# Down projection of the SwiGLU block: residual loads of a closing task ordered behind the first square sum of their tile group

## The chip, the cores and the metric

The kernel runs on one core of one Trainium2 chip. Five engines take part: TensorE (PE, with its weight loads as PEld), VectorE (DVE), ScalarE (ACT), GpSimd (POOL) and SyncE (SP), which issues nearly all of the DMAs here. The metric is the device time of one execution in microseconds. The kernel before took 3222.1 us (median of three runs, 3218.2 to 3226.84). The execution that was profiled took 3209.03 us.

## The reference

Two decoder layers run over 1024 positions of width 1024: a token mixer (gated spatial mixing in layer 0, an RWKV-7 recurrence in layer 1), a cross attention into 256 memory rows, and a SwiGLU block. Each is wrapped as `x + rms_norm(f(rms_norm(x)))`. The change lies in the SwiGLU block's second product and in the sum that follows it:

```python
def swiglu_ffn(x, w_in, w_out):
    gate, up = jnp.split(x @ w_in, 2, axis=-1)
    return (jax.nn.silu(gate) * up) @ w_out        # 2816 -> 1024

h = swiglu_ffn(rms_norm(x, g[4]), ffn_w_in[i], ffn_w_out[i])
x = x + rms_norm(h, g[5])                          # the "residual" is this x
```

## The kernel before

Products run in a split form: an operand is cut into a high and a low part (ACT casts, DVE subtracts: `split`, lines 118 and 119), and three matmuls of the parts replace one. In the SwiGLU block each product is further arranged as seven block products (a Strassen-like scheme). `ffn` (line 440) computes the hidden activations with the matmuls of L438, and `out(m)` inside it writes them to DRAM by SP in pieces `hd[1]` to `hd[7]` (L485 to L501; L490 and L491 store two of them for the last block before anything of the next part can be computed from it).

`ffn_out` (line 556 on) is the down projection. It goes through the products in the order 1, 2, 5, 6, 3, 7, 4, each in six steps (`steps`), with the matmuls of L639. For each step `load` fetches a piece of the hidden activations into a `wr` buffer (L596; there are three, and a buffer comes free when the low part of its split is done) and, in the first four products, a piece of `w_out` into an `a` buffer (L600). `evac` and `finish` take a product's result out of PSUM (L662 to L674), square and sum it on ACT (L651) and multiply it by the gain (L652). The output has eight row tiles of 128 rows. They close in groups: two tiles in layer 0 (`nn` is 2), one tile in layer 1. Even tiles get their first square sum at the end of product 2 and their last at the end of product 3. Odd tiles get them at the end of 7 and of 4. In layer 1 the last product runs tile by tile (`by_tile`).

When a group has all its square sums, `finish` puts a closing task in a queue: `close` (line 363). It loads the old rows of x, the residual, into `t` buffers (L369; there are four), forms the norm factor (L228 on DVE, L208 on POOL), adds the normed result to the residual (L378, DVE), stores the new rows (L379), and in layer 0 squares, scales and transposes them for the next block (L220, L389, L391, L262).

The order on each engine isn't the order of this code. A scheduler simulates the program and moves an instruction ahead when what it depends on is there. A residual load depends on nothing but a free `t` buffer and the rows of x in DRAM, so it may stand far ahead of the task that asks for it. SP issues in its order: where an issue waits, those behind it wait too.

After layer 0's down projection come the key and value product of the memory (L148 to L150, 256 columns wide) and then the recurrence of layer 1: `rwkv_prep` (L1318 to L1354), `rwkv_merge` (L1416, L1425) and `rwkv_chunks` (L1439, L1452), in four batches.

Of the kernel before, what the change touches and what calls it, by code (L numbers as in the profile page):

```python
# [21 lines left out]
class Trunk:  # L22
# [332 lines left out]
    def closer(self, gpost_row, xin, xout, gpre):  # L355

        nc = self.nc
        gpost = self.gain_bc(gpost_row)
        ready = [{}, {}]
        self.xT, self.hF = ({}, [])  # L360
        fp32_in, s7_in = (self.fp32_in, self.s7_in)

        def close(tiles, hs, s):

            n = len(tiles)
            xr = []
            for t in tiles:
                xr.append(self.tmp())
                nc.sync.dma_start(xr[-1], xin[t * P:(t + 1) * P, :])  # L369
            yield  # L370
            r = self.rms(s, n)
            yield
            s, s3 = self.sums(n)
            for i, t in enumerate(tiles):
                m = 2 if gpre is None and t == NT - 1 else 1
                for j in range(m):
                    js = slice(j * D // m, (j + 1) * D // m)
                    nc.vector.scalar_tensor_tensor(out=xr[i][:, js], in0=hs[i][:, js], scalar=r[:, i:i + 1], in1=xr[i][:, js], op0=ALU.mult, op1=ALU.add)  # L378
                    nc.sync.dma_start(xout[t * P:(t + 1) * P, js], xr[i][:, js])  # L379
                if gpre is not None:  # L380
                    self.sumsq(s3[:, :, i], xr[i])
                yield
            if gpre is None:
                return
            r = self.rms(s, n)
            yield
            for i in range(n):
                if 'avav'[i % 4] == 'a':
                    nc.scalar.activation(hs[i], xr[i], AF.Copy, scale=r[:, i:i + 1])  # L389
                else:  # L390
                    (nc.vector if 'avav'[i % 4] == 'v' else nc.gpsimd).tensor_scalar_mul(hs[i], xr[i], r[:, i:i + 1])  # L391
            yield
            half = tiles[0] // 4
            ready[half].update(zip(tiles, hs))
            if len(ready[half]) < 4:
                return
            self.fp32_in = fp32_in
            yield from (self.turn7 if s7_in else self.turn)(half, [ready[half][t] for t in sorted(ready[half])], gpre)
            ready[half] = None
        close.gpost, close.follow = (gpost, gpre is not None)  # L400
        return close
# [177 lines left out]
    def ffn_out(self, hd, w_out, mk_close, late):  # L579

        nc = self.nc
# [6 lines left out]
        y = {}  # L588
        close = mk_close()
# [43 lines left out]
        def mm(ps, q, j):  # L633
# [3 lines left out]
            for k in range(steps[n][1]):  # L637
                for z, (a, b) in enumerate(((hh[:, k, js], wh[:, k]), (hh[:, k, js], wl[:, k]), (hl[:, k, js], wh[:, k]))):
                    nc.tensor.matmul(ps, lhsT=a, rhs=b, start=i in (1, 2, 5) and n == 0 and k == 0 and z == 0, stop=n == NS - 1 and k == steps[n][1] - 1 and z == 2, skip_group_check=True)  # L639
        sums, done = ({}, {})  # L640

        def finish(t, c, src):

            group = (t % 2, t // 2 // nn)
            tiles = [2 * (group[1] * nn + g) + group[0] for g in range(nn)]
            if group not in sums:
                sums[group] = self.sums(nn)
                done[group] = 0
            s, s3 = sums[group]
            o = y[t][:, c * 512:c * 512 + 512]  # L650
            nc.scalar.activation(self.junk, src, AF.Square, scale=1.0 / 32, accum_out=s3[:, c:c + 1, tiles.index(t)])  # L651
            (nc.gpsimd if src is o else nc.vector).tensor_mul(o, src, close.gpost[:, c * 512:c * 512 + 512])  # L652
            done[group] += 1
            if done[group] == 2 * nn:
                self.later(close(tiles, [y[x] for x in tiles], s))

        def evac(i, j, A, B):
            o = lambda r, c: y[2 * j + r][:, c * 512:c * 512 + 512]
            if i in (1, 5):
                y[2 * j + i // 5] = self.a32()  # L660
            if i == 1:
                nc.scalar.copy(o(0, 0), A)  # L662
            elif i == 2:
                nc.vector.tensor_add(o(0, 0), B, o(0, 0))
                finish(2 * j, 0, o(0, 0))
            elif i == 5:
                nc.scalar.copy(o(1, 1), B)
            elif i == 6:
                nc.scalar.copy(o(0, 1), A)
            elif i == 3:  # L670
                nc.vector.tensor_add(o(0, 1), B, o(0, 1))
                finish(2 * j, 1, o(0, 1))
            elif i == 7:
                nc.vector.tensor_add(o(1, 1), A, o(1, 1))  # L674
                finish(2 * j + 1, 1, o(1, 1))
            else:
                finish(2 * j + 1, 0, A)
# [1055 lines left out]
```

## Time and profile before

| | |
|---|---|
| median of three runs | 3222.1 us (3218.2 to 3226.84) |
| profiled execution: time, span | 3209.03 us, 3207.3 us |
| mean granted TensorE clock | 0.972 |
| PE busy, share of the span | 3071.3 us, 96% |
| DVE, ACT, POOL busy | 57%, 46%, 28% |
| down projection, layer 0 | about 1082 to 1304 us of the span |
| recurrence batches, layer 1 | about 1800 to 2200 us |
| down projection, layer 1 | about 2979 us to the end |

PE is busy in nearly the whole span, so time is lost or won where PE waits, or where its granted clock is at the lower of its two levels. Other engines' idle time costs nothing in itself.

### The profile page before, as it was taken

To read this page: it belongs to the slowest core of one execution; us is meant where nothing else is said; L and a number is where in the kernel's file an instruction comes from. 1 tells how busy PE (TensorE), PEld (TensorE's weight loads), DVE (VectorE), ACT (ScalarE), POOL (GpSimd) and SP (SyncE) were. 2 spreads that over 40 slices of the span, in tenths; PEclk is the share of its full clock that TensorE was granted. 3 is DMA by queue.
4 is the path that set the end of the run, shared out by engine and by line. 5 is a ranking of instruction groups with operands and counts; after the bars stand their busy time and mean duration, and the time that the engine had idled before them with its cause. 6 is when DMAs were issued, how large, how long until landed. Compare 5 with 4: busy or idle time off the path is not lost. (4 is left out here: it accounts for less than half of the span.)

```text
span 3207.3 us, 44170 instructions
## 1 busy us (share of the span) xinstructions
PE 3071.3 (96%) x16570; PEld 2511.4 (78%) x16570; DVE 1829.9 (57%) x2674; ACT 1484.9 (46%) x2751; POOL 893.0 (28%) x762
## 2 busy tenths in 40 slices
PE   8999999999999999999989999999999899999998
PEld 6888888778888777878767788887788678888776
DVE  5553544574555476654775677654545755554566
ACT  5433544543333345666763355455545533333443
POOL 0100011365555200111331443333011555554001
PEclk9999999999999999999999889989999999999999
DMA  5622545413333643644867643535544233333634
GB/s 189 207 79 66 190 123 167 151 59 100 104 99 102 226 165 132 204 141 136 255 216 186 188 110 104 146 96 178 181 158 142 94 102 99 99 99 115 236 109 141
DMA packets 432502, 456.56 MB, mean 142 GB/s; under 512 B 77664, under 2 KB 307200, under 8 KB 432288
## 3 DMA queue, kind: packets, MB, share of 16 engines
q1 hardware_dynamic: 425376, 428.57, 42.1%
q0 software_dynamic: 6912, 25.17, 2.5%
q8 instruction: 131, 2.15, 0.3%
q14 instruction: 83, 0.68, 0.1%
HBM read 331.43 MB, written 122.22 MB: 141 GB/s over the span
## 5 line engine op out<-in xcount | busy, mean ns | idle before, releaser
L438 PE MATMUL ps<-a,wh 128*128 128x512 f32 x2464 | 772.0, 398 | 7.0 <-DVE a L119 4.8
L119 DVE TENSOR_TENSOR wl<-wr,wh 128x1024 fp32r<-128x1024 f32 (+1 forms) x417 | 477.6, 1155 | 480.1 <-ACT wh L118 477.3
L118 ACT CAST wh<-wr 128x1024 fp32r<-128x1024 f32 (+1 forms) x417 | 371.1, 901 | 621.3 <-PE ps L639 172.3
L438 PEld LDWEIGHTS ps<-a,wh 128*128 128x128 f32 x2464 | 465.3, 189 | 125.0 <-DVE a L119 7.1
L438 PE MATMUL ps<-a,wl 128*128 128x512 f32 x1232 | 480.2, 398 | 0.0
L148 PE MATMUL ps<-a,wh 128*128 128x512 f32 (+1 forms) x848 | 328.3, 392 | 11.2 <-ACT a L118 7.9
L149 PE MATMUL ps<-a,wh 128*128 128x512 f32 (+1 forms) x848 | 324.7, 384 | 2.4 <-DVE a L119 2.4
L208 POOL TENSOR_TENSOR sm<-sm,mhalf 128x4 f32<-128x4 f32 (+3 forms) x60 | 71.2, 1189 | 914.7 <-DVE sm L228 841.8
L148 PE MATMUL ps<-wh,a 128*128 128x512 f32 x800 | 314.5, 401 | 11.7 <-ACT t L1168 3.0
L150 PE MATMUL ps<-a,wl 128*128 128x512 f32 (+1 forms) x848 | 323.7, 383 | 1.5 <-DVE wl L119 1.5
L149 PE MATMUL ps<-wl,a 128*128 128x512 f32 x800 | 318.1, 398 | 0.8 <-DVE wl L119 0.8
L150 PE MATMUL ps<-wh,a 128*128 128x512 f32 x800 | 316.6, 399 | 0.0
L438 PEld LDWEIGHTS ps<-a,wl 128*128 128x128 f32 x1232 | 233.0, 189 | 57.2 <-DVE wl L119 0.9
L639 PE MATMUL ps<-wl,wh 128*128 128x512 f32 x588 | 231.9, 394 | 11.9 <-DVE wl L119 11.9
L119 DVE TENSOR_TENSOR wl<-s,wh 128x512 fp32r<-128x512 f32 x176 | 199.8, 1149 | 67.5 <-ACT wh L118 64.2
L639 PE MATMUL ps<-wh,wl 128*128 128x512 f32 x588 | 229.9, 391 | 0.0
L639 PE MATMUL ps<-wh 128*128 128x512 f32 x588 | 194.8, 394 | 13.2 <-ACT wh L118 13.2
L118 ACT CAST wh<-s 128x512 fp32r<-128x512 f32 x176 | 106.4, 620 | 199.7 <-PE ps L438 66.7
L148 PEld LDWEIGHTS ps<-a,wh 128*128 128x128 f32 x848 | 162.1, 192 | 44.3 <-ACT a L118 8.8
L150 PEld LDWEIGHTS ps<-a,wl 128*128 128x128 f32 x848 | 162.1, 191 | 35.7 <-DVE wl L119 2.8
L148 PEld LDWEIGHTS ps<-wh,a 128*128 128x128 f32 x800 | 151.3, 189 | 48.5 <-ACT t L1168 3.5
L149 PEld LDWEIGHTS ps<-a,wh 128*128 128x128 f32 x848 | 162.7, 192 | 32.6 <-DVE a L119 2.7
(281 smaller groups left out, 5426.2 us busy)
## 6 DMA issues: line engine op xcount, KB each, us to landing
scr<-a SPq DMA_DIRECT2D x218, 256.0 KB
wr<-in_ffn_w_in SPq DMA_DIRECT2D x90, 512.0 KB
wr<-scr SPq DMA_DIRECT2D x70, 512.0 KB
scr<-t SPq DMA_DIRECT2D x60, 512.0 KB
wr<-in_rw_w_rkv SPq DMA_DIRECT2D x48, 512.0 KB
a<-in_ffn_w_out SPq DMA_DIRECT2D x40, 512.0 KB
t<-scr SPq DMA_DIRECT2D x36, 512.0 KB
ld<-scr SPq DMA_DIRECT2D x72, 256.0 KB
```

The lines of the kernel that those rows point to most:

```text
L118: self.nc.scalar.copy(hi, src)
L119: (engine or self.nc.vector).tensor_sub(lo, src, hi)
L148: nc.tensor.matmul(out, lhsT=ah, rhs=bh, start=start, stop=False)
L149: nc.tensor.matmul(out, lhsT=ah, rhs=bl, start=False, stop=False)
L150: nc.tensor.matmul(out, lhsT=al, rhs=bh, start=False, stop=stop)
L208: self.nc.gpsimd.tensor_tensor(out=r, in0=v, in1=self.mhalf[:, 0:n], op=ALU.pow)
L438: self.nc.tensor.matmul(out, lhsT=a, rhs=b, start=start and k == 0 and (i == 0), stop=k == 3 and i == 2, skip_group_check=True)
L639: nc.tensor.matmul(ps, lhsT=a, rhs=b, start=i in (1, 2, 5) and n == 0 and k == 0 and z == 0, stop=n == NS - 1 and k == steps[n][1] - 1 and ...
```

## The change

`finish` remembers the column of the small tile into which the first square sum of a group goes, and hands it to `close`. There VectorE copies that column (128 x 1) into the first column of each `t` buffer, ahead of the load that overwrites the whole buffer. The load therefore comes after the copy, and the copy after the square sum of L651. Closing tasks of the other blocks pass no column and are as they were. There are 8 such copies in each layer's down projection, 16 in all. In the changed kernel all lines behind `close`'s loop have numbers that are two higher, and those behind `finish` three higher: L369, L485, L596 and L600 are there L371, L487, L598 and L602; L1318 to L1452 are L1321 to L1455.

```diff
-        def close(tiles, hs, s):
+        def close(tiles, hs, s, begun=None):
...
                 xr.append(self.tmp())
+                if begun is not None:
+                    nc.vector.tensor_copy(xr[-1][:, 0:1], begun)
                 nc.sync.dma_start(xr[-1], xin[t * P:(t + 1) * P, :])
...
-        sums, done = ({}, {})
+        sums, done, begun = ({}, {}, {})
...
                 done[group] = 0
+                begun[group] = sums[group][1][:, c:c + 1, tiles.index(t)]
...
-                self.later(close(tiles, [y[x] for x in tiles], s))
+                self.later(close(tiles, [y[x] for x in tiles], s, begun[group]))
```

What the scheduler makes of it is seen in three places. The first is SP's queue at the passage from the hidden activations to the down projection of layer 0 (`scr_93` is x, `scr_4980` to `scr_4986` are `hd`). Before:

```order
L596 DMA wr<-scr_4980 128x2x512 x2
L369 DMA t_9240<-scr_93 128x1024
L485 DMA scr_4980<-a 128x512
L596 DMA wr<-scr_4980 128x2x512
L369 DMA t_9242<-scr_93 128x1024
L369 DMA t_9332<-scr_93 128x1024
L490 DMA scr_4981<-a 128x512
L491 DMA scr_4983<-a 128x512
L600 DMA a<-in_ffn_w_out 128x512
```

Changed:

```order
L598 DMA wr<-scr_4980 128x2x512 x2
L487 DMA scr_4980<-a 128x512
L598 DMA wr<-scr_4980 128x2x512
L492 DMA scr_4981<-a 128x512
L493 DMA scr_4983<-a 128x512
L602 DMA a<-in_ffn_w_out 128x512
L497 DMA scr_4984<-a 128x512
```

The three residual loads are gone from here, and a fourth one, 14 rows further on, is gone too; the four stand some 30 rows later, between the hidden pieces of product 5. The rest keeps its order: the two stores still stand ahead of the first piece of `w_out`. Layer 1 has the same rows and the same move.

The second place is SP's queue near the end of layer 1's down projection (`scr_21280` and `scr_21277` are `hd[7]` and `hd[4]` before, `scr_21288` and `scr_21285` in the changed kernel; the stores are to the output). Before:

```order
L369 DMA t_25889<-scr_96 128x1024
L379 DMA out<-t_25577 128x1024
L596 DMA wr<-scr_21280 128x2x512
L369 DMA t_25933<-scr_96 128x1024
L379 DMA out<-t_25612 128x1024
L379 DMA out<-t_25656 128x1024
L596 DMA wr<-scr_21277 128x512
L369 DMA t_25977<-scr_96 128x1024
L369 DMA t_26021<-scr_96 128x1024
L596 DMA wr<-scr_21277 128x2x512 x5
```

Changed:

```order
L381 DMA out<-t_25586 128x1024
L598 DMA wr<-scr_21288 128x2x512
L381 DMA out<-t_25622 128x1024
L381 DMA out<-t_25667 128x1024
L598 DMA wr<-scr_21285 128x512
L598 DMA wr<-scr_21285 128x2x512 x5
L371 DMA t_25901<-scr_96 128x1024
L371 DMA t_25946<-scr_96 128x1024
L371 DMA t_25991<-scr_96 128x1024
L371 DMA t_26036<-scr_96 128x1024
```

The four last residual loads move from among the hidden pieces of products 7 and 4 to behind all of them.

The third place is on PE, in the third of the four recurrence batches, about where its chunk recurrence begins (L1452, changed L1455: state products; L1330, L1337 and L1354, changed L1333, L1340 and L1357: preparation of the next batch). Before:

```order
L1354 MATMUL ps<-uv,bk 64x64 x16
L1318 MATMUL ps<-sel,ld 128x2 x4
L1330 MATMUL ps<-ar,bk 128x128 x4
L1425 MATMUL ck<-z_14126,x1t 32x32
L1452 MATMUL ck<-s,ar 128x128 x3
L1330 MATMUL ps<-ar,bk 128x128 x4
```

Changed:

```order
L1357 MATMUL ps<-uv,bk 64x64 x8
L1428 MATMUL ck<-z_14134,x1t 32x32
L1357 MATMUL ps<-uv,bk 64x64
L1321 MATMUL ps<-sel,ld 128x2 x4
L1357 MATMUL ps<-uv,bk 64x64 x7
L1333 MATMUL ps<-ar,bk 128x128 x4
L1455 MATMUL ck<-s,ar 128x128 x3
L1333 MATMUL ps<-ar,bk 128x128 x4
```

The recurrence of this batch begins behind another 32 preparing matmuls of 64x64. The code of the recurrence is the same in both kernels: the scheduler's choices there shift with what came before. Of the 48 preparing matmuls of 64x64 that stood behind the start of this batch's recurrence 16 are left; in the first batch it is 16 instead of 32, in the second 48 instead of 32. PE has 14,412 matmul rows of order in both kernels.

## Rows read from the trace of the kernel before

**Rows 1.** The page: span, PE, and the chain that ended last.
```profile
span 3207.3 us, 44170 instructions
PE 3071.3 (96%) x16570; PEld 2511.4 (78%) x16570; DVE 1829.9 (57%) x2674; ACT 1484.9 (46%) x2751; POOL 893.0 (28%) x762
```
**Rows 2.** Timeline of SP, layer 0 passage: start us, us, engine line op.
```profile
1055.95 0.42 SPq L369 DMA_DIRECT2D t<-scr  x1
...
1062.19 12.23 SPq L369 DMA_DIRECT2D t<-scr  x2
1076.60 0.32 SPq L490 DMA_DIRECT2D scr<-a  x1
1076.97 0.42 SPq L491 DMA_DIRECT2D scr<-a  x1
1077.49 0.41 SPq L600 DMA_DIRECT2D a<-in_ffn_w_out  x1
```
**Rows 3.** Waits of SP, 1060 to 1080 us: total, times, longest.
```profile
SPq L369 <- POOL a L549: 11.3, 1, 11.3
...
SPq L490 <- DVE a L558: 2.1, 1, 2.1
```
**Rows 4.** Timelines of DVE, ACT and PE, the same passage; idle and releaser in brackets.
```profile
1075.88 0.69 DVE L558 TENSOR_TENSOR a<-t,ps 128x512 f32<-128x512 f32 x1 [2.73 <-issue]
...
1081.45 0.62 ACT L118 CAST wh<-a 128x512 fp32r<-128x512 f32 x1 [7.63 <-DMA a<-in_ffn_w_out]
...
1082.12 2.07 PE L639 MATMUL ps<-wh 128*128 128x512 f32 x4 [6.43 <-ACT wh L118]
...
1086.42 1.07 PE L639 MATMUL ps<-wh 128*128 128x512 f32 x4
```
**Rows 5.** Timeline of PE, the same passage in layer 1.
```profile
2979.06 2.07 PE L639 MATMUL ps<-wh 128*128 128x512 f32 x4 [6.42 <-ACT wh L118]
```
**Rows 6.** Timeline of SP, last products of layer 1.
```profile
3145.10 0.32 SPq L369 DMA_DIRECT2D t<-scr  x1
3145.59 1.53 SPq L379 DMA_DIRECT2D out<-t  x2
3148.00 0.33 SPq L596 DMA_DIRECT2D wr<-scr  x1
3150.66 1.56 SPq L369 DMA_DIRECT2D t<-scr  x2
3153.92 11.88 SPq L596 DMA_DIRECT2D wr<-scr  x5
```
**Rows 7.** The chain that ended last, in order of time, two stretches.
```profile
1998.85 2.37 DMA a<-scr
...
3148.00 4.47 DMA wr<-scr
...
3153.92 4.62 DMA wr<-scr
...
3162.03 4.64 DMA wr<-scr
...
3169.73 30.57 PE ps L639 x132
```
**Rows 8.** Timeline of PE, 3128 to 3170 us: rows with idle time before them.
```profile
3162.51 1.20 PE L639 MATMUL ps<-wh 128*128 128x512 f32 x4 [0.34 <-ACT wh L118]
3164.33 0.50 PE L639 MATMUL ps<-wl,wh 128*128 128x512 f32 x1 [0.62 <-DVE wl L119]
3169.73 0.50 PE L639 MATMUL ps<-a 128*128 128x512 f32 x1 [0.53 <-DVE a L674]
```
**Rows 9.** Timeline of DVE, the end of layer 1.
```profile
3173.66 0.68 DVE L652 TENSOR_TENSOR a<-a,gb 128x512 f32<-128x512 f32 x1
...
3184.62 1.29 DVE L378 SCALAR_TENSOR_TENSOR t<-a,sm,t 128x1024 f32<-128x1024 f32 x1 [0.66 <-POOL sm L208]
```
**Rows 10.** L228, 3130 to 3208 us: duration in ns, min/median/max, first and last start.
```profile
L228 DVE SCALAR_TENSOR_TENSOR sm<-sm x8: 150/152/156, 3133.6 to 3201.7; 128x1 f32<-128x1 f32 x8
```
**Rows 11.** Chain, recurrence of the last batch: a group of 42 at either clock level.
```profile
2154.80 6.00 PE ck L1439 x42
...
2164.73 3.51 PE ck L1439 x42
...
2170.81 3.51 PE ck L1439 x42
```
**Rows 12.** Windows: us, busy us of PE, PEld, DVE, ACT, POOL, PEclk, DMA share, GB/s.
```profile
1680.00:1840.00 160.00, 145.95 (x1107) 120.69 (x1106) 96.56 (x227) 60.16 (x104) 39.99 (x66) 0.91 0.69 192
1840.00:2000.00 160.00, 155.01 (x1692) 131.62 (x1691) 111.53 (x355) 84.83 (x249) 64.39 (x83) 0.89 0.38 102
2000.00:2200.00 200.00, 194.26 (x2044) 162.33 (x2044) 110.00 (x290) 101.66 (x286) 67.52 (x70) 0.90 0.43 118
```

## The prediction, made before the changed kernel ran

> **What bounds the kernel now.** I read the page first. PE is busy for 3071.3 of 3207.3 us [rows 1], so only what lengthens or shortens PE's own stretch can move the time. Then I looked at the two places in which the moved loads stand, with the timelines of SP, DVE, ACT and PE side by side, and last at the stretch of the recurrence, whose order moves though its code doesn't.
>
> At the passage into the down projection SP looks badly blocked. A pair of residual loads holds its queue for 12.23 us [rows 2], and 11.3 us of that is a wait for POOL's L549, the last reader of the `t` buffer [rows 3]. Behind that pair stand two stores of hidden activations and the first piece of `w_out`. PE waits 6.43 us in layer 0 and 6.42 us in layer 1 for the cast of just that piece [rows 4, 5]. So it is tempting to book the block as the cause of the wait. The reader is to look one row further: the store L490 starts at 1076.60, not at 1074.4 when the pair is through, and it waits for DVE's L558 [rows 3], which runs from 1075.88 for 0.69 us, to 1076.57 [rows 4]. L490 needs the last block of hidden activations, which PE and DVE finish no sooner. The residual pair is waited out inside a wait that stands anyway.
>
> At the end of layer 1 the chain that ended last runs through three loads of hidden pieces, of 4.47, 4.62 and 4.64 us, and then through 30.57 us of unbroken PE work [rows 7]. Two residual issues stand right among them in SP's queue [rows 6]. There DMA does reach PE.
>
> **The passages: what goes and what is late next.** Four residual loads leave each passage. SP's queue then goes from the hidden piece straight to L490, which still waits until 1076.57, and L491 and the `w_out` piece follow as before, at 1076.97 and 1077.49 [rows 2]. The load that was issued last, near 1074.4, has some 2 us before L490 starts and 3 us before the `w_out` piece, so little of it is still on the DMA engines; its share in the 3.96 us between the issue at 1077.49 and the cast at 1081.45 [rows 2, 4] is between 0 and, if it were all still in the way, half of that, 2 us. I take 0, since the two stores of 256 KB ahead of that piece and the loads behind it remain. For both layers that is 0, with 0 to -4 us for the range.
>
> **The end of layer 1.** Four residual loads move behind all hidden pieces. Without them the loads of 4.47 and 4.62 us have two stores beside them, and not these and two residual loads. The nearest short row of a load in the chain is 2.37 us [rows 7], for a smaller piece, so each may shrink by up to 2.2 us, and by nothing at worst. PE can take back only what it waits there: 0.34, 0.62 and 0.53 us [rows 8], 1.49 us in all. Even half of the 4.3 us on the loads covers that, so I take -1.5 us, with 0 as the other end. What is late next is PE itself: it has its 132 matmuls of the last product whatever the loads do.
>
> The moved loads have to be there for L378. In the tail the copies can run when VectorE has done the first gain product of each odd tile, at 3173.66 plus 0.68 for the first [rows 9]. With 0.4 us of issue [rows 2] and the longest load of the chain, 4.64 us [rows 7], the first residual is there at 3179.4; its L378 starts at 3184.62 [rows 9]. That is 5.2 us of cover, and the later tiles have more. In the even tiles the load goes out in product 5 and is used after product 3, three products later. If the cover were gone, each us of lateness in the last tile would be a us of the time; in the others PE would not notice.
>
> **The copies.** Sixteen copies of 128 x 1 are added on VectorE. Its nearest row is L228, also 128 x 1, at 0.152 us [rows 10]; 16 of them are 2.4 us. Most lie in VectorE's idle time. Some stand between the gain products and the splits that PE waits for next (six such places: the ends of products 2 and 7 in both layers, two of them twice). With two copies of 0.15 us on half of these I take +0.6 us. The ends are 0 and +2.4. Queued behind a copy that waits for ACT's square sum are VectorE's next evacuations and splits; but in the order each copy stands behind the gain product of the same or a later tile, when ACT's sum is already there, so I add no wait.
>
> **The recurrence.** Nothing is added or removed there, but PE's order changes in three of the four batches: the recurrence starts behind 32 more preparing matmuls in the third batch, 16 more in the first and 16 fewer in the second. The number of matmuls is the same. A price can't be read directly; I bound it by the clock. A group of 42 matmuls takes 3.51 us at the full level and 6.00 us at the lower one, and the period from one group to the next goes with it from 6.08 us (2164.73 to 2170.81) to 9.93 us (2154.80 to 2164.73) [rows 11]. One group per reordered batch that falls to the lower level, or rises from it, is 3 x 3.85 = 11.6 us, to either side. There is room for both: over 1840 to 2200 us the granted clock is about 0.9 and PE is busy in 349 of 360 us [rows 12], so it is at the lower level for about a fifth of the time. I take 0: two batches begin later, one earlier, and the work is the same.
>
> Here the Trainium skill has a rule that speaks against a reordering that opens gaps: TensorE: Matmul & The Clock Gate, section HAM oscillation, says that waits between bursts of matmuls make the engine slow down again, so that a gap costs more than its own length. The 2.07 us for four matmuls right after the 6.43 us wait, against 1.07 us for the same four later [rows 4], agree with it. By that rule the sum would lean to the slow side if the later starts open gaps, and would stay where it is if they only change places.
>
> **The sum.** On the profiled execution's own time: 3209.0 + 0 (passages) - 1.5 (tail) + 0.6 (copies) + 0 (recurrence) = 3208.1 us, a change of -0.9. That execution ran 13 us below the median of the runs, so I put the change on the median: 3222.1 - 0.9 = 3221 us.
>
> **Rivals.** *The block was the cause after all.* If the freed SP queue did let the first pieces of `w_out` go early, both waits of 6.4 us would go, and with them the slow restart, about 2 us each (1 us on the four matmuls just named, and as much on the next ones): 17 us, 3205 us. For it speaks the 12.23 us; against it that L490 stands ahead of the `w_out` piece in both orders and waits for L558.
>
> *The recurrence gets worse.* A later start leaves more of the recurrence without preparing matmuls to fill its pauses, and the clock falls: 11.6 us, 3233 us. It decides the result from about 10 us on, that is from two or three groups of 42 at the lower level. For it speaks that the two batches with later starts outnumber the one with an earlier start, and that the last batch, which has no filling, is where the slow groups stand now [rows 11]; against it that PE is busy throughout.
>
> *The recurrence gets better.* The same price with the other sign: 3209 us. For it: the lower level takes a fifth of that stretch, and less interleaving could also mean fewer breaks.
>
> *The moved loads come late.* If the copies waited long in VectorE's queue, the last residual would hold the last L378; with 5 us of cover at the first tile and more than 20 at the last this needs a delay that no row shows. The time would still be within a few us of 3222.
>
> **Chances.** My forecast, no change that can be seen, 0.62 (own range 3215 to 3228, the spread of single runs and the small terms); the block was the cause 0.07; recurrence worse 0.17; better 0.12; late loads 0.02, which I count as no change. A measurement here can tell about 0.3%, 9.7 us, from no change. With that, faster by more is 0.19, within 0.64, slower by more 0.17. The range that should hold the time 8 times in 10 reaches into both recurrence cases: 3210 to 3233 us.
>
> **What would show it.** In the changed profile: SP's long issue of residual loads gone at both passages, yet L490 (there L492) still starting right behind L558 and PE still waiting about 6.4 us; at the end of layer 1 the first two loads of the last product under 4 us and PE's three small waits gone; the last residuals landing before 3184. Wrong would be a wait at the passages of 4 us or less (then the block was the cause), or a recurrence stretch whose length moves by more than 5 us, which would set the result alone.

## The result and the profile after

The changed kernel is slower: 3241.42 us (median of 20 executions, 3223.34 to 3259.34) against 3223.6 us for the kernel before in the same sessions (3212.82 to 3249.73, 20 executions). The ratio is 1.0052, with a 95% interval of 1.0034 to 1.0070. The prediction was 3221 us and no change; the time lies above its range.

Where the change was made, the profile after looks as predicted. First the sixteen copies, as the page of line L370 gives them (duration in ns, min/median/max, first and last start):

```profile
L370 DVE COPY t<-sm x16: 143/150/160, 1144.3 to 3211.8; 128x1 f32<-128x1 f32 x16
```

SP's queue at layer 0's passage, then what the store waits for (total, times, longest), then PE's waits for the first `w_out` piece in layer 0 and in layer 1:

```profile
1062.49 0.36 SPq L598 DMA_DIRECT2D wr<-scr  x1
1077.35 0.33 SPq L492 DMA_DIRECT2D scr<-a  x1
1077.74 0.43 SPq L493 DMA_DIRECT2D scr<-a  x1
1078.27 0.38 SPq L602 DMA_DIRECT2D a<-in_ffn_w_out  x1
```
```profile
SPq L492 <- DVE a L560: 14.4, 1, 14.4
```
```profile
1082.81 2.08 PE L641 MATMUL ps<-wh 128*128 128x512 f32 x4 [6.40 <-ACT wh L118]
3013.93 2.07 PE L641 MATMUL ps<-wh 128*128 128x512 f32 x4 [5.87 <-ACT wh L118]
```

The residual block of 12.23 us is gone [rows 2], and nothing came of it. The wait that was booked on the residual loads, 11.3 us, and the 2.1 us of the store behind them [rows 3] stand now as one wait of 14.4 us in the store's name. PE's waits are 6.40 and 5.87 us, against 6.43 and 6.42 [rows 4, 5].

At the end of layer 1 the four last residual loads stand behind all hidden pieces (SP), behind the copy, and are there before the first L380 asks for them (DVE, which waits only for POOL's factor):

```profile
3184.07 15.30 SPq L598 DMA_DIRECT2D wr<-scr  x6
3207.14 5.18 SPq L371 DMA_DIRECT2D t<-scr  x4
```
```profile
3206.96 0.15 DVE L370 COPY t<-sm 128x1 f32<-128x1 f32 x1
3217.42 1.29 DVE L380 SCALAR_TENSOR_TENSOR t<-a,sm,t 128x1024 f32<-128x1024 f32 x1 [0.66 <-POOL sm L208]
```

PE waits there once, for 2.72 us at 3177.06, which the kernel before also does (2.71 us at 3141.01); the three small waits of [rows 8] are gone. The first load of the last product is cast 2.8 us after its issue (3184.07 to 3186.90), where it was 4.55 (3148.00 to 3152.55). From the matmul behind the wait of 2.7 us to the end it is 66.3 us before and 64.0 after. That gain of 2.3 us doesn't show in the larger stretch, from the first matmul of layer 1's hidden product to the end (689.7 us before, 2517.62 to 3207.3, and 689.8 after, 2551.26 to 3241.1), since this execution had lost about as much before that matmul.

Up to 1580 us, behind all that layer 0's half of the change moves, PE's records in the two profiles stay within 2 us of each other.

The time went in the recurrence, which no line of the change touches. The four batches, each from the start of its merge to the next (us, PE busy and records, granted clock, DMA share, GB/s), before and after:

```profile
1821.60:1900.90 79.30, 74.12 (x964) 0.91 0.45 123
1900.90:2009.20 108.30, 104.48 (x1137) 0.85 0.44 118
2009.20:2131.50 122.30, 118.77 (x1232) 0.97 0.50 135
2131.50:2197.30 65.80, 65.79 (x733) 0.77 0.23 68
```
```profile
1827.00:1914.00 87.00, 76.13 (x964) 0.88 0.43 116
1914.00:2026.00 112.00, 108.53 (x1136) 0.83 0.43 114
2026.00:2159.90 133.90, 130.53 (x1233) 0.86 0.45 123
2159.90:2226.00 66.10, 66.10 (x733) 0.77 0.23 68
```

375.7 us became 399.0. In the first batch PE is idle for 5.7 us more (10.9 against 5.2); in the second and third it is busy all the same, with as many records, at a lower granted clock. These 23.3 us are the larger part of the 33.8 us between the two spans; 5.4 us more lie ahead of the first merge, which starts anywhere from 1821.6 to 1830.3 us in executions of the order of before. One execution of each can't say which of these differences is the order's and which is chance. That took the experiments.

### The profile page after: what moved, and what is told of

The parts are those of the page before. It is cut to its first block, busy times and chain, and to the rows that moved or that the text cites. A ratio compares the mean times of both kernels' runs of the same rounds, so it can differ in the third digit from the quotient of the medians.

```text
span 3241.1 us, 44205 instructions
## 1 busy us (share of the span) xinstructions
PE 3095.0 (95%) x16570; PEld 2530.7 (78%) x16570; DVE 1835.8 (57%) x2690; ACT 1484.3 (46%) x2751; POOL 889.7 (27%) x762
## 5 line engine op out<-in xcount | busy, mean ns | idle before, releaser
L641 PE MATMUL ps<-wl,wh 128*128 128x512 f32 x588 | 232.2, 395 | 11.5 <-DVE wl L119 11.3
```

## The experiments

All ratios are to the kernel before on the same chip, with 95% intervals; 12 executions of each kernel, 35 of the kernel before per session.

**One layer at a time.** Layer 1 alone:

```diff
-                self.later(close(tiles, [y[x] for x in tiles], s, begun[group]))
+                self.later(close(tiles, [y[x] for x in tiles], s, None if close.follow else begun[group]))
```

> Only layer 1's closing tasks get the column; layer 0 and the recurrence stand in the order of before on every engine, and layer 1's last product in that of the changed kernel. Theory A (the loss comes from the recurrence, whose order follows from layer 0's half of the change): ratio to before 1.000, at most 0.0005 lower (the 1.5 us of the three waits in the tail), and recurrence batches as in before, the first with about 2.5 us of idle PE. Theory B (the later loads and the copies cost where they stand): half of the loss, 1.0026.

Measured: 0.9985 (0.9959 to 1.0012). In its profile PE is idle in the first batch for 4.8 us, near the 5.2 us of the kernel before, and not about 2.5.

Layer 0 alone:

```diff
-                self.later(close(tiles, [y[x] for x in tiles], s, begun[group]))
+                self.later(close(tiles, [y[x] for x in tiles], s, begun[group] if close.follow else None))
```

> Only layer 0's closing tasks get the column; everything up to layer 1's last product stands in the changed kernel's order on every engine. Theory A: the whole loss, ratio 1.005 (3240 us), with the first recurrence batch some 7 us longer by a PE wait of about 6 us for VectorE's mask product, and the third longer at a lower clock. Theory B: half of it, 1.0026.

Measured: 1.0058 (1.0028 to 1.0087). The whole loss comes with layer 0's half, and theory B, which shares it between the layers, falls. Of the two details expected, the third batch came (148.7 us, clock 0.77), the first did not: 82.2 us.

**The order alone, with the loads left as they are.** Eight small copies on ScalarE at the start of layer 1's mixer shift the scheduler's choices. In the changed kernel:

```diff
         nc = self.nc
+        nc.scalar.copy(self.junk[:, 0:128], self.ident)
...
         B = [self.rwkv_batch() for _ in range(4)]
```

> The changed kernel with 8 small ScalarE copies (128x128, into the unused square tile) ahead of layer 1's mixer. They cost nothing that PE waits for (8 x 0.2 us on ScalarE), but the order of the second half of the recurrence comes out another way: the third batch begins behind 24 preparing matmuls of 64x64 instead of 48; the first batch keeps the changed order. If the first batch's start costs by its order and the third by its own: the first batch keeps its 7 us, the third loses its 11.5 us, ratio 1.0015 to 1.003. If the third batch's length is chance of the clock or follows from the first: 1.005. If the copies' nudge does nothing and layer 0's loads cost: 1.005 with the first batch at 79 us.

Measured: 1.0002 (0.9974 to 1.0029). The same eight lines in the kernel before:

> The kernel before with the same 8 small ScalarE copies. Residual loads as before. The first batch keeps the order of before (16 preparing matmuls of 64x64 ahead), the second and third begin behind 25 each instead of 32 and 16. If the recurrence's order sets the time whatever the loads do: the first batch 79 us with 2.5 us idle, and a time that moves by the length of the second and third, anywhere from 0.998 to 1.005; if only the loads matter: 1.000 and batches as in before.

Measured: 1.0048 (1.0022 to 1.0073). This pair decides against the loads: with the whole change in place the loss can vanish, and without any of it, it can come. In detail the expectation of the nudged changed kernel was only half met: the ratio lies below each of the three that were named, the third batch stayed at 131.7 us, and the second was shorter (105.4 us). In the nudged kernel before the first batch came as expected (79.5 us), and the second and third took 114.8 and 134.0 us.

**The third batch alone.** One 64x1 copy in the changed kernel that depends on a late step of the second batch:

```diff
             nc.scalar.copy(uvc, u)
+            if (b, c4, p) == (1, 3, 0):
+                for _ in range(1):
+                    nc.vector.tensor_copy(self.small(1)[0:64], uvc[:, 0:1])
```

> The changed kernel with one VectorE copy of a 64x1 column more, which waits for a late step of the second batch's recurrence. Every engine keeps the changed order up to there (the first batch and nearly all of the second); the third batch then begins behind 16 preparing matmuls of 64x64, as in the kernel before, instead of 48. Theory A (the order of the third batch sets most of the loss, by the granted clock): the third batch falls from 134 to 149 us to about 122, and the ratio to before from 1.005 to 1.000 to 1.002. Theory B (the loss comes from layer 0's loads, or the first two batches): 1.004 to 1.006, with a third batch of 130 us or more.

Measured: 0.9994 (0.9973 to 1.0014). The loss is gone, with the loads, the copies, and the order of every engine up to late in the second batch as in the changed kernel. The third batch did not come down to 122 us but to 130.2: the ratio is that of theory A, the length that of theory B, and the table below shows how far the third batch accounts for it.

**Is it the count of preparing matmuls ahead?** In the kernel before:

```diff
             nc.scalar.copy(uvc, u)
+            if (b, c4, p) == (0, 3, 0):
+                for _ in range(1):
+                    nc.scalar.copy(self.junk[0:64, 0:128], uvc)
```

> The kernel before with one small ScalarE copy (64x128) more, late in the first batch's recurrence. The loads stand as before; the third batch begins behind 32 preparing matmuls of 64x64 instead of 16, and the end of the first batch is a little otherwise. If the number of preparing matmuls ahead of the third batch sets its length: 130 us or more for it and a ratio of 1.002 to 1.004. If not: 122 us and 1.000.

Measured: 0.9987 (0.9964 to 1.0010). The premise did not come true: PE's 16,570 records in the profile of this kernel stand in the order of the kernel before, one for one by name and shape, with the same 369 from the third merge to the first state product (L1452), in 21.1 us. So the run says nothing on the count of preparing matmuls, which stays untested. It is a repeat of the order of before, with the same time. Its one profile was a long execution (3236.54 us, against a median of 3217.68), with 133.4 us for the third batch: that order, too, can have a long third batch. What I counted from here on is the time and PE's records from the third merge to its first state product.

**Does denser work hold the clock?** Ahead of each merge, here in the changed kernel, then in the kernel before:

```diff
+        for i in range(8):
+            nc.tensor.matmul(pb[i % 4], lhsT=self.chunk_on[:, 0:128], rhs=self.chunk_on, start=True, stop=True)
         for h in range(2):
             for c in range(8):
```

> The changed kernel with 8 bf16 matmuls (128x512, of a constant by itself, overwritten at once) ahead of each merge of the recurrence, 32 in all, of about 0.22 us each: 7 us of added work, part of it in pauses ahead of the merges. The order moves too: 32, 16 and 16 preparing matmuls ahead of the batches. If the lower clock after the merges comes from thin PE work around them and denser work holds the clock: the low stretches that start at the merges (73 to 82 us of lost time in the two profiles with the changed order) shrink by 20 us or more, ratio 0.998 to 1.000. If the fill does nothing for the clock: as the third-batch kernel plus up to 7 us, 1.002 to 1.005.

Measured: 1.0016 (0.9999 to 1.0034). That lies between the two ranges. It can't be set against the changed kernel, because its third batch was put in another order as well. Against the third-batch kernel, which has as many records (401) from the third merge to its first state product, its median is 8.0 us longer, about the added work.

> The kernel before with the same 32 filling matmuls; the batches begin behind 16, 32 and 16 preparing matmuls as before. If denser work around the merges holds the clock: 0.994 to 0.998, with less than 40 us lost to the lower level between the mixer and the end of the recurrence (51 and 53 us in the two profiles with this order). If it does nothing: up to 7 us of added work, 1.000 to 1.002.

Measured: 1.0008 (0.9988 to 1.0028), with 54.5 us lost to the lower level in its profile, not under 40. Its mean clock over the executions is 0.9683 against 0.9669, and its added work takes back as much. But the order moved here too: 401 records and 35.6 us stand from the third merge to its first state product, not 369 and 21.0. So neither filled kernel tests the filling by itself; in neither does it show a gain.

**More executions of the same orders.** To tell order from chance, the changed kernel twice more and the kernel before twice more:

> The changed kernel, profiled once more, for where in the recurrence the lower clock lies. If the third batch's order sets the loss: the third batch again 130 us or more, with 30 us or more at the lower level in it. If the place is chance: its loss lies in another batch.

> As the run before it: third batch 130 us or more if its order sets the loss; another place if the place is chance.

> The kernel before, profiled once more. If the third batch's order sets the loss: its third batch again about 122 us, with some 10 us at the lower level behind its merge. If the place is chance: 130 us or more in one of the two repeats.

> As the run before it: 122 us if the order sets it; the other batches may move by 10 us to either side, as they did between the two profiles of this order so far (the fourth 65.8 and 57.2 us).

and the third-batch kernel twice more:

> The third-batch kernel, profiled once more. Its one profile had a third batch of 130.2 us, between the means of the order of before (122.9 us of four profiles) and of the changed one (140.2 us of four). If the third batch's order takes the loss away by its own length: 122 to 131 us again, and never near 148.7. If its time was even for another reason: 134 us or more here and other batches shorter.

> As the run before it: a third batch of 122 to 131 us if its own order takes the loss away.

With the layer-1 kernel and the kernel with one more ScalarE copy (the recurrence's order is that of before in both) and the layer-0 kernel (the changed order) there are five profiles of the order of before, four of the changed one, and three of the third-batch kernel. Length of each batch, us (the fifth value of the order of before is the long execution just named):

| batch | order of before | changed order | third-batch kernel |
|---|---|---|---|
| first | 79.3, 84.8, 87.8, 88.2, 90.4 | 87.0, 82.2, 83.9, 82.8 | 79.1, 83.6, 82.1 |
| second | 108.3, 106.1, 106.6, 104.6, 106.6 | 112.0, 114.9, 105.7, 107.3 | 107.2, 107.4, 101.4 |
| third | 122.3, 122.1, 121.6, 125.4, 133.4 | 133.9, 148.7, 129.4, 148.7 | 130.2, 129.5, 129.7 |
| fourth | 65.8, 57.2, 67.2, 61.6, 70.1 | 66.1, 57.6, 66.2, 57.5 | 63.8, 62.2, 55.1 |
| mean of the sum | 381.9 | 396.0 | 377.1 |

The third batch is the one that differs most: means of 125.0 and 140.2 us, 15.2 us apart, where the medians of the executions are 17.8 us apart. Its values overlap in one profile, the 133.4 us. The first batch's longer idle time in the changed kernel's profile is no part of it. The second batch's mean is 3.5 us longer in the changed order, on values that overlap. The third-batch kernel's sum is 18.9 us below the changed one's; 10.4 us of that lie in the third batch, the rest in batches whose values overlap.

Two expectations of the repeats fell short: the first repeat of the changed kernel had 129.4 us, not 130, with 23.6 us at the lower level, not 30, and the second of the kernel before had 125.4 us, not 122, with a second stretch of 10 us at the lower level.

The third batch, cut at its first state product, in the kernel before, the changed one and the layer-0 kernel (columns as above):

```profile
2009.20:2030.20 21.00, 21.00 (x369) 0.81 0.63 162
2030.20:2131.50 101.30, 97.77 (x866) 1.00 0.47 129
```
```profile
2026.00:2072.00 46.00, 45.62 (x529) 0.75 0.65 182
2072.00:2159.90 87.90, 84.92 (x706) 0.92 0.35 92
```
```profile
2020.10:2080.60 60.50, 60.21 (x529) 0.53 0.51 146
2080.60:2168.80 88.20, 85.12 (x705) 0.93 0.32 84
```

In the changed order 160 more records stand ahead of the state products, and 160 fewer behind. Work only changed places, and the part behind is 13 us shorter. But the part ahead is 25.0 and 39.5 us longer, since it runs at a low granted clock. Length times granted clock, an estimate of the same work at the full level, is 17.0 + 101.3 = 118.3 us before, 34.5 + 80.9 = 115.4 us in the changed kernel, 32.1 + 82.0 = 114.1 us in the layer-0 kernel. By that estimate the changed order would be no longer at one clock. The repeats fall on the same two lengths, 46.4 and 60.5 us; the order of before gives 20.9 to 21.5 us every time.

In the layer-0 kernel, around the second fall (columns as above, then PE's rows there):

```profile
2020.10:2045.00 24.90, 24.61 (x276) 0.50 0.60 170
2045.00:2049.00 4.00, 4.00 (x30) 0.93 0.35 108
2049.00:2093.00 44.00, 44.00 (x282) 0.50 0.35 99
2093.00:2168.80 75.80, 72.72 (x650) 1.00 0.36 96
```
```profile
2041.22 3.67 PE L1357 MATMUL ps<-uv,bk 128*64 128x64 f32 x32
2044.82 1.35 PE L1321 MATMUL ps<-sel,ld 128*128 128x2 f32 x8
2046.10 1.16 PE L1333 MATMUL ps<-ar,bk 64*128 64x128 f32 x8
2047.19 0.24 PE L1428 MATMUL ck<-z,x1t 32*32 32x32 f32 x2
2047.36 1.16 PE L1333 MATMUL ps<-ar,bk 64*128 64x128 f32 x8
2048.45 0.75 PE L1340 MATMUL ps<-ident,bk 128*128 128x128 f32 x4
2049.13 2.07 PE L1333 MATMUL ps<-ar,bk 64*128 64x128 f32 x8
```

Eight records of L1333 take 1.16 us at 2047.36 and 2.07 us at 2049.13. The clock falls between them, with no idle time before any of these rows, and stays at the lower level for 44 us in which PE is busy for 44.00. (The profile models the ends of matmuls, so it can't rule out short pauses inside a row.) The changed kernel's own profile ran the same 282 records, in the same order, at the full level:

```profile
2054.00:2078.85 24.85, 24.85 (x282) 1.00 0.64 171
```

The two repeats split the same way, 24.86 and 43.97 us. So the stretch can go either way, and when it falls that costs 19.1 us. The lower level makes these records 43.96 / 24.85 = 1.77 times as long. With this factor the account closes better than with the clock alone. The third batch spent 7.7 to 8.6, 19.2 and 32.1 us at the lower level in the five profiles of the order of before, and 23.6, 36.8, 69.7 and 69.7 us in the four of the changed one. Taking back what these stretches cost by that factor leaves, as an estimate, 117 to 119 us in all nine. The third batch differs by its time at the lower level and by nothing else that can be seen.

## Why the prediction was wrong, point by point

**What held.** The passages: SP's long wait was only a wait inside a wait; 0 was taken, and PE's waits moved by 0.03 and 0.55 us. The tail: the three small waits went, and the end came out 2.3 us shorter in the profile, where 1.5 was taken. The copies: 16 of 0.15 us, hidden or nearly so (PE's wait behind the last two of layer 0 is 6.47 us, and 6.41 without them). The loads came in time. The third-batch kernel has all of this and differs from the kernel before by 0.9994 (0.9973 to 1.0014); the forecast for these terms, -0.9 us, is 0.9997. The rival of the block as the cause is out, and so is that of the late loads.

**The step that failed** is "The recurrence: I take 0: two batches begin later, one earlier, and the work is the same." The work is the same, and one batch, the third, costs 15 us more on the mean, by the account above all of it time at the lower level. The rival "the recurrence gets worse" is what happened, though not by its mechanism. It was given 0.17 and the price 11.6 us; the medians moved by 17.8 us. The prediction had named the sign itself: a recurrence stretch that moves by more than 5 us. It moved by 23.3 us in the profile.

Two things in that step were wrong. The bound was one group of 42 matmuls per batch, 3.85 us each [rows 11], taken from the slowest place that the profile before showed. But the reordering made the stretch from the third merge to its first state product 46 to 60 us long, and the bound left it out. The profile before has a stretch of this kind, in its second batch, and the prediction did not read it:

```profile
1900.90:1942.80 41.90, 41.76 (x473) 0.66 0.56 154
```

This is the part from the second merge to its first state product, with 104 more records than the third batch had there. It lost 41.9 x 0.34 = 14.2 us to the lower level, and the third 21.0 x 0.19 = 4.0 us. By these rows 104 more records cost some 10 us, an estimate, where the prediction took 3.85 us for each reordered batch. And the place was wrong. The rival spoke of a recurrence left without filling, so that its pauses grow. The part behind the start has less filling, indeed, and is shorter, at a clock of 0.92 to 1.00. It is the gathered filling, ahead of the start, that runs slowly.

By the rule of the Trainium skill that the prediction weighed (TensorE: Matmul & The Clock Gate, HAM oscillation), the sum would lean to the slow side if the later starts opened gaps. The time did come out slower, and the trace agrees with the rule in part. In all nine profiles of the two orders the clock first falls near the third merge, in or within 3 us behind a wait of PE of 1.0 to 1.3 us. But that wait stands in both orders, and PE's waits in the third batch add up to 3.1 us before and 3.9 us after. What differs is how long the lower level then lasts: 10 us in the five profiles of the order of before, 24 to 31 us in the four of the changed one. And the second fall in the layer-0 kernel, with 44.00 of 44.00 us busy, follows no wait that the profile shows.

**The chances.** I counted starts: two later, one earlier. The first batch's later start cost nothing (means 86.1 and 84.0 us), so counting was no argument. The second mistake of method was to set terms of 1 us against a single profiled execution: executions of this kernel spread over 37 us, and one batch in one order moves by 10 us and more between them (the fourth: 57.2 to 70.1 us).

**What stays open.** Why the granted clock stays low in one execution and recovers in another, in the same stretch with the same order (46.4 and 60.5 us), and which property of the work ahead of the state products it is: no run tested the count of preparing matmuls, and the filled kernels, whose order moved as well, didn't settle it. How much of the third-batch kernel's gain is the third batch's, on three profiles. Why the nudged kernel before is as slow as the changed kernel with 427 records from the third merge to its first state product (43.3 us), when the nudged changed kernel has 417 (39.3 us) and is not slow: a longer second batch in its one profile (114.8 against 105.4 us) points to a part there, which was not tested by itself. Nor was it tried why the scheduler, some 700 us later, orders the third batch otherwise after layer 0's loads have moved.

## What to carry to other kernels

Where a scheduler orders the program, a small edit is an edit of everything behind it: compare the order of all engines to the end, and price each stretch that changes, not only the place of the edit. Where a stretch grows (here: a long run of small matmuls ahead of the products they prepare), look in the trace of before for the nearest one of its new form, in another batch if need be, and let the range leave room for the whole stretch at the lower clock. And before one order is called better, a control that shifts the order without the edit, and one that has the edit without the shift, are worth more than a closer look at the edit.

## What the runs showed that was not expected

The differences between executions and between kernels go with one thing: the granted clock. Span times mean granted clock, averaged over each kernel's executions:

| kernel | ratio | mean clock | span x clock, us |
|---|---|---|---|
| before (70 executions) | 1 | 0.9669 | 3115.5 |
| changed (20) | 1.0052 | 0.9618 | 3116.1 |
| layer 1 only (12) | 0.9985 | 0.9683 | 3113.2 |
| layer 0 only (12) | 1.0058 | 0.9617 | 3116.5 |
| nudged, changed (12) | 1.0002 | 0.9667 | 3114.9 |
| nudged, before (12) | 1.0048 | 0.9622 | 3113.3 |
| third batch only (12) | 0.9994 | 0.9663 | 3112.7 |
| order of before, one more ScalarE copy (12) | 0.9987 | 0.9683 | 3116.3 |
| filled, changed (12) | 1.0016 | 0.9660 | 3120.7 |
| filled, before (12) | 1.0008 | 0.9683 | 3123.3 |

The product is the same within 0.13% for all kernels without filling, whatever their time, and 5 and 8 us higher with 32 filling matmuls. The kernels with a ratio of about 1.005 have a mean clock of 0.962, the others 0.966 to 0.968. And a PE that the profile shows as busy need not be at the upper level: 282 records of small matmuls, with no idle time between them, ran at the lower one for 44 us in two executions and at the upper one for 25 us in two others.
